# First MLP product of a two-layer backbone: sums moved from GpSimd to VectorE, operand 2 split earlier, context's products put together

## The chip, the core and the metric

The kernel runs on one core of a Trainium2 chip. The metric is the device time of one execution in microseconds; three runs gave 2661.84 to 2663.42, median 2663.18. The core's engines work side by side, each through its own queue in order: TensorE (PE; its weight loads are listed as PEld) multiplies matrices and writes to PSUM, VectorE (DVE) and ScalarE (ACT) do elementwise work, GpSimd (POOL) does elementwise work on SBUF only, and SyncE (SP) issues DMAs. Semaphores order the engines among each other.

## The reference, cut to what matters

Two layers, window attention and gated linear attention, each followed by an MLP, on 1024 latent tokens and, in the first layer, 256 context tokens of width 1024. All is fp32.

```python
def channel_mlp(h, w_in, w_out):
    return jnp.square(jax.nn.relu(h @ w_in)) @ w_out

for i in range(DEPTH):                       # DEPTH = 2
    need_ctx = i < DEPTH - 1
    m_lat = jnp.split((c_lat @ w_mod[i] + b_mod[i])[:, None, :], N_MOD, axis=-1)
    m_ctx = jnp.split(c_con @ w_mod[i] + b_mod[i], N_MOD, axis=-1)
    ...
    x_lat = x_lat + m_lat[2] * rms_norm(y_lat, g_post_mix[i])
    f_lat = channel_mlp(modulate(x_lat, g_pre_mlp[i], m_lat[3], m_lat[4]), w_mlp_in[i], w_mlp_out[i])
    x_lat = x_lat + m_lat[5] * rms_norm(f_lat, g_post_mlp[i])
    if need_ctx:                             # the same for x_ctx
        ...
```

`w_mlp_in[i]` is 1024 x 4096; the product `h @ w_in` is the first MLP product. `modulate` is a norm, a factor and a shift per column.

## The kernel before, in words

**Operands.** An fp32 operand is used in two parts: `split` writes a rounded high part (ScalarE, L213, a cast) and the rest as a low part (VectorE, L214, a subtraction), and `mm3` adds three matmuls, high by high, low by high and high by low (L233 to L235).

**First MLP product** (`mlp_hidden`). The latent tokens are two halves of four tiles of 128, the inner dimension has two halves, and the hidden columns come in 16 blocks `m` of two times 128. Each block is a two-by-two product done with seven products instead of eight. Product `j` (1 to 7) multiplies operand `j` of the activations (`x.ops[j]`, rows `o1` to `o7` of the trace, split once by `MlpIn.apart`) with operand `j` of the weights (rows `wi`, split for each block). Some operands are sums: `sums(m, j)` makes four sums of weight quarters for each block (128x512, L891), on GpSimd; `MlpIn.take` makes those of the activations tile by tile (L131, L132), and `last_sums` turns two operands into sums in place once products 1 and 2 no longer need them (L228 through the helper `sums`: one half on VectorE, the other on GpSimd). A product fills or adds to a PSUM bank (`pa`, `pb`, `pc`). ScalarE copies a bank (L932), VectorE adds another to the copy (L936, an eviction sum), ScalarE applies relu and square (L937, L894).

In layer 0 the context's 256 tokens go through plain products in addition: `x0` for the first 128 columns of a block, `x1` for the second (rows `px`).

**PSUM.** `ps1` has four buffers of one bank; `ps2` has two of two banks, which `y`, `pb`, `px` and, once `tight` is set, the transposes `xt` take in turns. `modulated` transposes a tile on TensorE and evicts the eight 128x128 pieces in turns on ScalarE (L449) and VectorE (L451).

**The entry.** Before the MLP, `mixing` runs over the token tiles: output product `y`, post norm and residual (L462, L463), norm (L429), transposition and modulation (L449, L451), sums (L131, L132). The last tiles of it overlap the first products of the MLP: products 1 and 2 of the first blocks (two blocks in layer 0, three in layer 1) need operands of the first half of the tokens only, product 6 needs the last tile.

**Modulation.** `mod_sums` multiplies `w_mod` by the two conditioning vectors on VectorE: for each 128 rows a tile `wm` of 512 KB is loaded, and each of one or two streams adds to an accumulator `ma` (L313, L315). In layer 0's first MLP product its 56 units are called at even distances.

**What sets the order.** `Timeline` holds a plan: each step is put at a planned time (`tl.at`), a product counting 2.56, and the program is emitted in the order of these times. A scheduler then sets each engine's final order from the emitted one. On the chip each engine takes its queue in that order.

## Time and profile before

| | |
|---|---|
| median of three runs | 2663.18 us |
| the profiled execution | 2665.38 us |
| its span, first to last instruction | 2663.7 us |
| mean granted TensorE clock | 0.988 |
| TensorE busy | 2565.3 us (96%) |
| VectorE busy | 1706.7 us (64%) |
| ScalarE busy | 1258.7 us (47%) |
| GpSimd busy | 638.5 us (24%) |

Layer 0's first MLP product begins at 640.8 us of the span, layer 1's at 2014.4. In a timeline a row gives the start, the duration, the engine, the line, the operation, the tiles written and read, the shape and a count; in brackets stands the idle time of the engine before it and what ended it. Neighbouring instructions overlap by some hundredths of a microsecond, so that the distance of two starts is a little less than a duration. A matmul's row lasts longer than the distance to the next, since they are pipelined. The granted clock is a share of the full rate: 1.00 is the level of 2.4 GHz, 0.50 that of 1.2 GHz.

### The profile page before, as it was taken

The page shows a single profiled execution, that of the slowest core. Times are in us where ns is not written, and L with a number is a line of the kernel's source. Part 1 is how long each engine was busy: PE and PEld are TensorE (multiplying, and loading weights), DVE is VectorE, ACT ScalarE, POOL GpSimd, SP SyncE. Part 2 cuts the span into 40 slices and gives each one's busy share as a digit, 9 for nine tenths or more (in the row PEclk, how much of TensorE's full clock was granted, in tenths as well). Part 3 has the DMA queues.
Part 4 walks back from the last instruction along what each step waited for, and adds up shares of the span by engine and source line. Part 5 has one row for each costly group of instructions (what it writes and reads, how often), then busy time and mean ns, then how long its engine had stood idle before and what let it go on. Part 6 is the DMA issues. An engine that isn't in the chain of part 4 may idle for free. (4 is left out here: it accounts for less than half of the span.)

```text
span 2663.7 us, 36464 instructions
## 1 busy us (share of the span) xinstructions
PE 2565.3 (96%) x13523; PEld 2125.0 (80%) x13523; DVE 1706.7 (64%) x2531; ACT 1258.7 (47%) x2364; POOL 638.5 (24%) x868
## 2 busy tenths in 40 slices
PE   7998999999999999999998999999997999999998
PEld 5777888887788888788776888888786888878787
DVE  4798766657867554866758634736647454478786
ACT  3325777744544444543325544433435454545333
POOL 0355655423223221000001112312414232300002
PEclk9999999999999999999998999999998999999999
DMA  9221000222555654646345322002221434376464
GB/s 305 89 70 40 4 2 25 72 87 74 151 181 172 186 181 147 232 157 226 115 150 197 109 51 91 25 24 95 88 94 42 127 108 114 119 244 212 168 213 166
DMA packets 223523, 329.76 MB, mean 124 GB/s; under 512 B 23897, under 2 KB 122481, under 8 KB 223345
## 3 DMA queue, kind: packets, MB, share of 16 engines
q1 hardware_dynamic: 220752, 318.00, 37.2%
q0 software_dynamic: 2592, 9.44, 0.9%
q8 instruction: 106, 1.74, 0.3%
q14 instruction: 73, 0.59, 0.1%
HBM read 267.60 MB, written 59.77 MB: 123 GB/s over the span
## 5 line engine op out<-in xcount | busy, mean ns | idle before, releaser
L234 PE MATMUL p<-ol,oh 128*128 128x512 f32 x896 | 350.9, 392 | 1.7 <-DVE ol L214 1.7
L235 PE MATMUL p<-oh,ol 128*128 128x512 f32 x896 | 347.1, 391 | 0.0
L233 PE MATMUL p<-oh 128*128 128x512 f32 x896 | 333.0, 394 | 6.7 <-DVE acc L1123 3.7
L246 POOL TENSOR_SCALAR rs<-ss 128x1 f32<-128x1 f32 (+1 forms) x78 | 25.8, 331 | 981.5 <-ACT later L240 796.9
L233 PEld LDWEIGHTS p<-oh 128*128 128x128 f32 x896 | 170.0, 190 | 44.4 <-ACT oh L213 4.7
L234 PEld LDWEIGHTS p<-ol,oh 128*128 128x128 f32 x896 | 169.6, 189 | 38.8 <-DVE ol L214 2.9
L235 PEld LDWEIGHTS p<-oh,ol 128*128 128x128 f32 x896 | 169.3, 189 | 35.5 <-issue 0.2
L315 DVE SCALAR_TENSOR_TENSOR ma<-wm,cT,ma 128x1024 f32<-128x1024 f32 x112 | 162.8, 1486 | 45.1 <-DMA wm<-in_w_mod 44.9
L214 DVE TENSOR_TENSOR ol<-wh,oh 128x1024 fp32r<-128x1024 f32 x128 | 153.7, 1216 | 54.5 <-ACT oh L213 51.3
L214 DVE TENSOR_TENSOR wi<-wi,wi 128x512 fp32r<-128x512 f32 x176 | 154.7, 910 | 49.5 <-ACT wi L213 47.5
L213 ACT CAST oh<-wh 128x1024 fp32r<-128x1024 f32 x128 | 132.4, 1052 | 107.8 <-PE p L235 45.5
L213 ACT CAST oh<-k 128x1024 fp32r<-128x1024 f32 x96 | 98.5, 1053 | 152.4 <-PE p L235 65.3
L932 ACT COPY s<-pa 128x512 f32<-128x512 f32 x96 | 56.1, 586 | 199.4 <-PE pa L235 199.4
L936 DVE TENSOR_TENSOR s<-pc,s 128x512 f32<-128x512 f32 x64 | 43.9, 686 | 162.5 <-ACT s L932 145.5
L710 DVE CUSTOM_DVE_ANT_0 pr<-sc,mask,nsink 128x640 f32<-128x640 f32 (+2 forms) x144 | 108.5, 775 | 42.7 <-PE sc L699 40.9
L214 DVE TENSOR_TENSOR ol<-k,oh 128x1024 fp32r<-128x1024 f32 x96 | 115.4, 1219 | 26.4 <-ACT oh L213 16.4
L715 ACT ACTIVATE pr<-pr,nm 128x640 f32<-128x640 f32 (+2 forms) x160 | 118.6, 742 | 28.1 <-DVE nm L710 25.0
L727 POOL TENSOR_SCALAR pr<-pr,den 128x640 f32<-128x640 f32 (+2 forms) x160 | 118.1, 752 | 36.4 <-PE pt L743 16.8
L235 PE MATMUL y<-woh,ol 128*128 128x512 f32 x288 | 112.5, 391 | 2.8 <-DVE ol L214 2.8
L213 ACT CAST wi<-wi 128x512 fp32r<-128x512 f32 x176 | 102.5, 614 | 26.4 <-DMA hd<-h 7.9
L233 PE MATMUL y<-woh,oh 128*128 128x512 f32 x288 | 114.0, 396 | 0.0
L234 PE MATMUL y<-wol,oh 128*128 128x512 f32 x288 | 112.3, 390 | 0.0
(374 smaller groups left out, 6974.4 us busy)
## 6 DMA issues: line engine op xcount, KB each, us to landing
wm<-in_w_mod SPq DMA_DIRECT2D x96, 512.0 KB, 4.4
wh<-hd SPq DMA_DIRECT2D x160, 256.0 KB, 3.5
wh<-in_w_mlp_out SPq DMA_DIRECT2D x160, 256.0 KB, 4.1
wi<-in_w_mlp_in SPq DMA_DIRECT2D x64, 512.0 KB, 5.6
hd<-h SPq DMA_DIRECT2D x64, 512.0 KB, 3.3
k<-hd SPq DMA_DIRECT2D x64, 256.0 KB, 5.3
k<-in_w_mlp_out SPq DMA_DIRECT2D x64, 256.0 KB, 5.4
x<-in_x SPq DMA_DIRECT2D x16, 512.0 KB, 3.6
```

What stands on the lines that cost most here:

```text
L213: self.nc.scalar.copy(hi, src)
L214: self.nc.vector.tensor_tensor(lo, src, hi.bitcast(F32), op=ALU.subtract)
L233: mm(out, a[0], b[0], start=start, stop=False, skip_group_check=onto)
L234: mm(out, a[0], b[1], start=False, stop=False, skip_group_check=onto)
L235: mm(out, a[1], b[0], start=False, stop=stop, skip_group_check=onto)
L246: nc.gpsimd.tensor_scalar(r, ss, inv_n, EPS, ALU.mult, ALU.add)
L315: nc.vector.scalar_tensor_tensor(acc[s], raw, c, acc[s], ALU.mult, ALU.add)
L710: nc.vector.tensor_tensor_reduce(out=like(pr), in0=like(ps[e][:, off:768]), in1=mask, scale=1.0, scalar=self.nsink[:, c0 + e : c0 + e + 1] ...
L715: nc.scalar.activation(pr, pr, AF.Exp, bias=nm[:, e : e + 1], scale=-1.0, accum_out=sums[:, e : e + 1])
L727: nc.gpsimd.tensor_scalar(probs[e], probs[e], den[:, e : e + 1], 0.0, ALU.mult, ALU.add)
L932: nc.scalar.copy(s["s", j], s["pa"])
L936: nc.vector.tensor_tensor(t, s[bank], t, op=ALU.add)
```

## The change

Six edits. (1) The four weight sums of a block move from GpSimd to VectorE. (2) So do the halves of `last_sums` that ran on GpSimd; the helper `sums` goes. (3) The split of activation operand 2 is planned at `t0 - 7`, ahead of the last tile's tail, where it stood at `at[0, 2] - 6`, which was -0.88 in layer 0 and 1.68 in layer 1. (4) In layer 0, for the first two blocks, `x1` follows `x0` directly and so stands ahead of product 6; for the others it follows product 3 as before. (5) With it the weight operand 3 of these blocks is split in time for `x1`, and sum 4 keeps its place. (6) `mod_sums` gives back control after each stream instead of each unit, so 80 calls replace 56, planned from 36 instead of 30 on.

```diff
@@ MlpIn.last_sums
             if j == 1:
-                kb.sums(c, raw[0, 0][c], m, raw[0, 0][c], ALU.add)
+                kb.nc.vector.tensor_tensor(raw[0, 0][c], m, raw[0, 0][c], op=ALU.add)
             else:
-                kb.sums(c, raw[0, 1][c], raw[0, 1][c], m, ALU.subtract)
+                kb.nc.vector.tensor_tensor(raw[0, 1][c], raw[0, 1][c], m, op=ALU.subtract)
@@ Backbone
-    def sums(self, c, out, a, b, op):
-
-        (self.nc.gpsimd if c else self.nc.vector).tensor_tensor(out, a, b, op=op)
@@ mod_sums
-    def mod_sums(self, vectors):
+    def mod_sums(self, vectors, apart=False):
...
                     nc.vector.scalar_tensor_tensor(acc[s], raw, c, acc[s], ALU.mult, ALU.add)
+                if apart and s + 1 < len(streams):
+                    yield
@@ mlp_hidden
                 full.append((m, j))
-                if full[-1] == (m, j) and j in (1, 2) and (m, 3 - j) in full:
+                if j in (1, 2) and (m, 3 - j) in full:
                     full.append((m, "x0"))
-                if j == 3:
+                    if m < g:
+                        full.append((m, "x1"))
+                if j == 3 and m >= g:
                     full.append((m, "x1"))
...
-            nc.gpsimd.tensor_tensor(out, p, q, op=op)
+            nc.vector.tensor_tensor(out, p, q, op=op)
...
             when = {j: at[m, j] - lead for j in range(1, 8)}
+            if x.ctx:
+                when[3] = min(when[3], at[m, "x1"] - lead)
...
-            tl.at(min(when[4], when[3]) - 2, lambda m=m: sums(m, 4))
+            tl.at(min(when[4], at[m, 3] - lead) - 2, lambda m=m: sums(m, 4))
...
-            tl.at(at[0, 2] - 6, lambda c=c: x.apart(2, c))
+            tl.at(t0 - 7, lambda c=c: x.apart(2, c))
@@ run
-        more = self.mod_sums([(0, 5)] + [(1, j) for j in range(6)])
+        more = self.mod_sums([(0, 5)] + [(1, j) for j in range(6)], True)
...
-        for n in range(56):
-            tl.at(30 + n * (t1 - 60) / 56, lambda: next(more))
+        for n in range(80):
+            tl.at(36 + n * (t1 - 60) / 80, lambda: next(more))
```

Two engines show what this does to the order. In the changed file the lines above the middle are numbered up to four lower, so L449 there is L451 of before, L427 is L429, L311 is L315, and L229 to L231 are L233 to L235. (A name's last number tells buffers apart.)

VectorE in layer 1's entry, before: from the normalisation of the last tile (`xn`) to the fourth VectorE eviction of the transpose buffer `xt_18153` (`q_3247`), whose release product 2 waits for.

```order
L429 TENSOR_SCALAR xn_18174<-xo_18127,rs_18177 128x1024
L214 TENSOR_TENSOR o2l_18182<-q_3182_17564,o2h_18181 128x1024
L214 TENSOR_TENSOR o2l_18186<-q_3183_17565,o2h_18185 128x1024
L214 TENSOR_TENSOR wi_3283_18189<-wi_18023,wi_3283_18189 128x512
L214 TENSOR_TENSOR wi_3286_18207<-wi_18114,wi_3286_18207 128x512
L214 TENSOR_TENSOR wi_3291_18249<-wi_18118,wi_3291_18249 128x512
L214 TENSOR_TENSOR wi_3295_18270<-M_18247,wi_3295_18270 128x512
L451 TENSOR_SCALAR q_3246_17980<-xt_18153,G_10146,S_9703 128x128
L451 TENSOR_SCALAR q_3243_17969<-xt_18225,G_10146,S_9703 128x128
L132 TENSOR_TENSOR qM_17986<-q_3246_17980,q_3243_17969 128x2x128
L131 TENSOR_TENSOR q_3243_17969<-q_3179_17553,q_3243_17969 128x2x128
L451 TENSOR_SCALAR q_3247_17981<-xt_18153,G_10146,S_9703 128x128
```

The same place after the change, up to the same eviction (of `xt_18161`); ahead of the first row stand the normalisation, the splits `wi_3286` and `wi_3291` and one sum (`M_18247`).

```order
L891 TENSOR_TENSOR wi_18023<-wi_18024,M_18247 128x512
L891 TENSOR_TENSOR M_18268<-wi_18115,wi_18114 128x512
L891 TENSOR_TENSOR M_18292<-wi_18119,wi_18118 128x512
L214 TENSOR_TENSOR wi_3295_18270<-M_18247,wi_3295_18270 128x512
L891 TENSOR_TENSOR wi_18114<-wi_18115,M_18268 128x512
L449 TENSOR_SCALAR q_3246_17980<-xt_18161,G_10314,S_10015 128x128
L449 TENSOR_SCALAR q_3243_17969<-xt_18225,G_10314,S_10015 128x128
L891 TENSOR_TENSOR wi_18118<-wi_18119,M_18292 128x512
L891 TENSOR_TENSOR M_18247<-wi_18023,M_18247 128x512
L132 TENSOR_TENSOR qM_17986<-q_3246_17980,q_3243_17969 128x2x128
L131 TENSOR_TENSOR q_3243_17969<-q_3179_17553,q_3243_17969 128x2x128
L449 TENSOR_SCALAR q_3247_17981<-xt_18161,G_10314,S_10015 128x128
```

The two splits of operand 2 have left this stretch, for a place ahead of the evictions of the tile before; the split `wi_3283` stands ahead of the normalisation; seven sums have come in.

TensorE in layer 0's entry, before, at the last tile's transposes (`xt`), which follow product 2 (`pb`) and `x0` (`px`) of the first block:

```order
L235 MATMUL px_7272<-ah_6403,wi_1517_7181 128x256
L441 MATMUL xt_7300<-ident,xn_7222 128x128 x4
L441 MATMUL xt_7309<-ident,xn_7222 128x128 x4
L233 MATMUL pb_7329<-o2h_7173,wi_1527_7244 128x512
L234 MATMUL pb_7329<-o2l_7174,wi_1527_7244 128x512
L235 MATMUL pb_7329<-o2h_7173,wi_1527_7244 128x512
```

And after the change:

```order
L231 MATMUL px_7272<-ah_6403,wi_1517_7181 128x256
L439 MATMUL xt_7297<-ident,xn_7222 128x128 x4
L439 MATMUL xt_7306<-ident,xn_7222 128x128 x4
L229 MATMUL px_7322<-ah_6402,wi_1518_7184 128x256
L230 MATMUL px_7322<-al_6404,wi_1518_7184 128x256
L231 MATMUL px_7322<-ah_6402,wi_1518_7184 128x256
```

Here 24 matmuls of the first block's `x1` have moved in ahead of the second block's product 2; the second block's `x1` follows its `x0`, and product 6 comes after them.

VectorE in layer 0's steady part, before, at a place where four modulation steps stand together ahead of an eviction sum (L936):

```order
L339 TENSOR_TENSOR S_8423<-S_8423,bcol 128x8
L315 SCALAR_TENSOR_TENSOR ma_8450<-wm_8496,cT,ma_8450 128x1024
L315 SCALAR_TENSOR_TENSOR ma_8451<-wm_8496,cT,ma_8451 128x1024
L315 SCALAR_TENSOR_TENSOR ma_8450<-wm_8540,cT,ma_8450 128x1024
L315 SCALAR_TENSOR_TENSOR ma_8451<-wm_8540,cT,ma_8451 128x1024
L936 TENSOR_TENSOR s_1713_8542<-pc_8508,s_1713_8542 128x512
```

And a piece of the same stage after it:

```order
L891 TENSOR_TENSOR wi_7703<-wi_7704,M_7891 128x512
L311 SCALAR_TENSOR_TENSOR ma_7620<-wm_7844,cT,ma_7620 128x1024
L311 SCALAR_TENSOR_TENSOR ma_7621<-wm_7844,cT,ma_7621 128x1024
L936 TENSOR_TENSOR s_1611_7790<-pc_7792,s_1611_7790 128x512
L311 SCALAR_TENSOR_TENSOR ma_7620<-wm_7913,cT,ma_7620 128x1024
L311 SCALAR_TENSOR_TENSOR ma_7621<-wm_7913,cT,ma_7621 128x1024
L936 TENSOR_TENSOR s_1628_7923<-pb_7830,s_1628_7923 128x512
```

In the whole stage the modulation steps now stand alone or in pairs, and the sums stand between them. Outside the two stages the queues are as before, but for some twenty rows at the end of layer 0's second MLP product, where TensorE's last pairs of transposes, and the splits and evictions around them, stand a few rows later or earlier.

## Rows read from the trace of the kernel before

**Rows 1.** The page, busy time by engine: us, share of the span, instructions.

```profile
PE 2565.3 (96%) x13523; PEld 2125.0 (80%) x13523; DVE 1706.7 (64%) x2531; ACT 1258.7 (47%) x2364; POOL 638.5 (24%) x868
```

**Rows 2.** The table by stretches (us from the span's start): length, then busy time and count of PE, PEld, DVE, ACT and POOL, the granted clock, the DMA engines' share and GB/s. Layer 0's entry and steady part, layer 1's entry and steady part, the end of layer 0's second MLP product.

```profile
640.00:702.00 62.00, 54.44 (x265) 44.26 (x266) 55.22 (x63) 38.64 (x68) 25.46 (x18) 0.97 0.27 79
702.00:1040.00 338.00, 332.76 (x1776) 284.39 (x1775) 209.32 (x241) 155.77 (x297) 81.98 (x51) 0.99 0.57 176
2014.00:2060.00 46.00, 32.23 (x125) 25.10 (x126) 38.84 (x44) 26.17 (x45) 22.02 (x15) 0.85 0.03 12
2060.00:2340.00 280.00, 278.82 (x1226) 229.48 (x1225) 127.39 (x152) 144.92 (x262) 79.27 (x52) 1.00 0.40 122
1424.00:1466.00 42.00, 31.19 (x129) 23.74 (x128) 34.41 (x52) 26.53 (x50) 9.12 (x14) 0.84 0.62 214
```

**Rows 3.** The timeline of TensorE in layer 1's entry: the end of product 1, the transposes, and the start of product 2.

```profile
2022.62 0.40 PE L235 MATMUL pa<-o1h,wi 128*128 128x512 f32 x1
2022.85 1.03 PE L441 MATMUL xt<-ident,xn 128*128 128x128 f32 x8
2034.11 0.79 PE L233 MATMUL pb<-o2h,wi 128*128 128x512 f32 x1 [10.22 <-DVE q L451]
```

**Rows 4.** The timeline of VectorE at the same place.

```profile
2019.96 1.78 DVE L429 TENSOR_SCALAR xn<-xo,rs 128x1024 f32<-128x1024 f32 x1 [0.77 <-ACT o2h L213]
2021.66 4.51 DVE L214 TENSOR_TENSOR o2l<-q,o2h 128x1024 fp32r<-128x1024 f32 x2
2026.10 4.01 DVE L214 TENSOR_TENSOR wi<-wi,wi 128x512 fp32r<-128x512 f32 x3
2030.04 0.68 DVE L214 TENSOR_TENSOR wi<-M,wi 128x512 fp32r<-128x512 f32 x1
2030.64 0.72 DVE L451 TENSOR_SCALAR q<-xt,G,S 128x128 f32<-128x128 f32 x2
...
2033.66 0.72 DVE L451 TENSOR_SCALAR q<-xt,G,S 128x128 f32<-128x128 f32 x2
```

**Rows 5.** The timeline of GpSimd at the same place.

```profile
2022.85 4.45 POOL L891 TENSOR_TENSOR M<-wi,wi 128x512 f32<-128x512 f32 x2
2027.26 1.71 POOL L891 TENSOR_TENSOR wi<-wi,M 128x512 f32<-128x512 f32 x1
2030.79 1.27 POOL L891 TENSOR_TENSOR M<-wi,M 128x512 f32<-128x512 f32 x1 [1.83 <-DVE wi L214]
```

**Rows 6.** The table by stretches (columns as in rows 2) at three places where the granted clock falls.

```profile
656.00:660.80 4.80, 4.72 (x15) 3.75 (x16) 3.74 (x7) 4.16 (x10) 3.19 (x3) 0.64 0.09 27
2034.10:2039.20 5.10, 5.09 (x12) 4.02 (x13) 0.94 (x3) 0.00 (x0) 0.00 (x0) 0.50 0.01 3
779.60:783.00 3.40, 3.37 (x8) 2.69 (x9) 1.29 (x2) 2.98 (x6) 0.58 (x1) 0.51 0.00 1
```

**Rows 7.** The timeline of VectorE in layer 0's entry: instructions one after the other.

```profile
633.24 0.75 DVE L429 TENSOR_SCALAR xn<-xo,rs 128x1024 f32<-128x1024 f32 x1 [2.14 <-POOL rs L247]
633.91 0.72 DVE L451 TENSOR_SCALAR q<-xt,G,S 128x128 f32<-128x128 f32 x2
634.55 0.41 DVE L131 TENSOR_TENSOR q<-q,q 128x256 f32<-128x256 f32 x1
634.88 0.41 DVE L451 TENSOR_SCALAR q<-xt,G,S 128x128 f32<-128x128 f32 x1
...
662.75 1.21 DVE L228 TENSOR_TENSOR q<-qM,q 128x1024 f32<-128x1024 f32 x1
663.88 1.21 DVE L228 TENSOR_TENSOR q<-q,qM 128x1024 f32<-128x1024 f32 x1
```

**Rows 8.** The timeline of TensorE in layer 0's entry: the rows with idle time before them, and two neighbouring rows of the context's product.

```profile
656.08 0.50 PE L233 MATMUL pb<-o2h,wi 128*128 128x512 f32 x1 [2.12 <-DVE s L936]
...
661.01 0.28 PE L234 MATMUL px<-al,wi 128*128 128x256 f32 x1
661.13 0.28 PE L235 MATMUL px<-ah,wi 128*128 128x256 f32 x1
...
666.61 0.50 PE L234 MATMUL pa<-o6l,wi 128*128 128x512 f32 x1 [1.14 <-DVE o6l L214]
...
670.52 0.50 PE L234 MATMUL pa<-o6l,wi 128*128 128x512 f32 x1 [0.87 <-DVE o6l L214]
...
674.46 0.50 PE L234 MATMUL pa<-o7l,wi 128*128 128x512 f32 x1 [1.15 <-DVE o7l L214]
```

**Rows 9.** The timelines of VectorE and of TensorE in layer 0's steady part, at two eviction sums.

```profile
770.85 2.48 DVE L315 SCALAR_TENSOR_TENSOR ma<-wm,cT,ma 128x1024 f32<-128x1024 f32 x2 [0.63 <-DMA wm<-in_w_mod]
...
774.45 4.53 DVE L315 SCALAR_TENSOR_TENSOR ma<-wm,cT,ma 128x1024 f32<-128x1024 f32 x2
...
779.63 0.80 PE L233 MATMUL pc<-o3h,wi 128*128 128x512 f32 x1 [2.26 <-DVE s L936]
...
804.21 4.86 DVE L315 SCALAR_TENSOR_TENSOR ma<-wm,cT,ma 128x1024 f32<-128x1024 f32 x4
...
809.72 0.50 PE L233 MATMUL pc<-o3h,wi 128*128 128x512 f32 x1 [1.50 <-DVE s L936]
```

**Rows 10.** Groups of VectorE's instructions by line: count, busy us, mean ns of one, idle time before them and what ended it. The first is of 702 to 1040, the second of 2060 to 2340.

```profile
L315 DVE SCALAR_TENSOR_TENSOR ma<-wm,cT,ma 128x1024 f32<-128x1024 f32 x66 | 95.3, 1470 | 37.6 <-DMA wm<-in_w_mod 37.5
...
L214 DVE TENSOR_TENSOR wi<-wi,wi 128x512 fp32r<-128x512 f32 x70 | 74.3, 1104 | 1.4
```

## Prediction

> **What bounds the kernel now.** I read the page's busy times first: TensorE is busy for 2565.3 of the 2663.7 us, so 98 us of idle time, and what the clock takes, are all that an edit off TensorE can win [rows 1]. Then a table by stretches, for where that idle time lies in the two stages that the change touches: 7.6 us in the entry of layer 0's first MLP product (640 to 702), 5.2 in its steady part, 13.8 in the entry of layer 1's (2014 to 2060), 1.2 in its steady part [rows 2]. That is 27.8 us, the ceiling but for the clock. Then the timelines of TensorE and VectorE at those places. The reader is to see that each long wait there ends with a VectorE instruction, and that VectorE is late because its queue is in order and its instructions are stretched.
>
> In layer 1 TensorE stops at 2023.88, after the second half of a transpose, until 2034.11 [rows 3]. Product 2 takes the PSUM buffer of that transpose, so it waits for the last of the buffer's evictions (L451). Those stand in VectorE's queue behind the split of operand 2 and four weight splits, which take 4.51 and 4.01 us and 0.68 [rows 4], while GpSimd runs sums on the same tiles [rows 5]. When TensorE resumes, the granted clock is 0.50, the 1.2 GHz level, and the 5.1 us of matmuls up to 2039.2 cost half of that, 2.5 us [rows 6].
>
> **The shared port.** A 128x512 split takes 0.68 us alone and two splits of 128x1024 took 4.51 beside GpSimd's sums, against 1.21 for one 128x1024 instruction in layer 0 [rows 4, 7]; GpSimd's two sums took 4.45 meanwhile [rows 5]. The Trainium skill, "SBUF — State Buffer", section "Who interferes with whom", says that a VectorE instruction with two SBUF inputs and a GpSimd instruction that reads SBUF exclude each other for the whole instruction, and that the loser stops. By it the stretched rows fall back to their lone durations once GpSimd is idle, as I assume below; if the stretch came from something else, the two splits would keep 4.5 us. The trace agrees as far as these rows go: the stretched splits lie beside GpSimd's sums, and the one that stands in a pause of them took 0.68 [rows 4, 5].
>
> **The change part by part.**
>
> *a, layer 0's entry.* The losses are four waits, 2.12, 1.14, 0.87 and 1.15 us [rows 8], and 3.4 us at 1.2 GHz around 657 [rows 6], half of it lost: 5.3 + 1.7 = 7.0. The change puts context's second product of the first two blocks, 48 matmuls of 0.12 us (5.8 us) [rows 8], ahead of product 6, and splits operand 2 while VectorE is idle. Walk it. TensorE has 48 matmuls at 0.23 [rows 3], 96 at 0.12 and 16 transposes (two times 1.03) before product 6: 24.6 us from 640.8, so it arrives at 665.4. VectorE's queue from 640.3 to operand 6's first low part holds, by its order: 19 instructions of 128x512 (splits, moved sums, two eviction sums), whose starts lie 0.60 apart, 16 small ones at 0.32 to 0.34, six of 128x1024 at 1.13 and a normalisation at 0.75 [rows 4, 7]. That is 11.4 + 5.3 + 6.8 + 0.75 = 24.2 us, and 1.21 for the low part itself: it is there at 665.7. Nearly even. I leave 1.0 us for two restarts and for VectorE waiting on ScalarE between evictions: a = -6.0. If VectorE loses 2 us to such waits and the clock dips again, -3; at best -7.
>
> *b, layer 0's steady part.* Two waits of 2.26 and 1.50 us, each for an eviction sum (L936) behind modulation steps: two that took 4.53 us, four that took 4.86 [rows 9]. A lone pair takes 2.48, so the first of them lost 4.53 - 2.48 = 2.05 to the stretch [rows 9]. After the change no more than two stand together in the whole stage, by the order, so both waits should nearly go, with the 1.7 us of the clock dip at 779.6 [rows 6]: 2.05 of the one, the 1.50 of the other and 1.7 = 5.2. What is added: four sums in each of 14 blocks, 56 of 0.60, 34 us, minus the stretch of 66 steps (1470 ns against the 1240 of one in the lone pair, 15 us) [rows 9, 10], on an engine that was busy for 209 of 338 us [rows 2]. Busy time fits; order is the question, since an eviction sum may now stand behind a sum and a pair that waits for its weights. The moved step gives its load less time: a load starts after the second stream's step, and by the plan in the code the next step comes 308/80 = 3.85 us later instead of 308/56 = 5.5; the loads make VectorE wait already. I charge 2.2 us for new waits: b = -3.0. Bounds -6.9 (all idle time and the dip) and +4 from here; the larger case is a rival.
>
> *c, layer 1's entry.* VectorE now runs, from the normalisation (L429) to the last eviction that frees the buffer: 0.75, two splits, four sums, a split, a sum, two evictions, two sums, two small ones and the eviction, that is ten at 0.60, two at 0.32, two at 0.34 and 0.41, together 8.5 us, where before it took 14.1 (2019.96 to 2034.07) [rows 4, 7]. One split more and one sum more now stand before the normalisation, 1.2 us, of which the 0.77 us of idle time there takes the larger part [rows 4]. So TensorE resumes between 2028.5 and 2029.6 instead of at 2034.1: 5.0 us. The split of operand 2 saves 4.4, the lone durations and the split that stands earlier save 5.4, and the seven sums in this queue give 4.2 back. The low clock after the wait I leave as it is, since TensorE still stands for about 5 us. Behind it, VectorE's work between the first eviction sum and operand 6's first low part gains two sums of 1.13 (those that GpSimd did, L228) and one of 0.60, and loses the stretch of the splits; I count no change. c = -5.0; bounds -1 (the sums also delay product 1's low parts) and -14 (all idle time of the entry).
>
> *d, layer 1's steady part.* 1.2 us is all there is. 70 splits shrink from 1104 to 680 ns, 30 us, and 56 sums add 34 [rows 4, 10]; VectorE stays near 130 of 280 us [rows 2]. 0, bounds -1 and +2.
>
> *e, the end of layer 0's second product.* The order moves one pair of transposes there by some eight matmuls, in a stretch with 10.8 us of idle time [rows 2]. +1, bounds -1 and +2.
>
> The moved loads are the same in number; GpSimd keeps only the small sums of the norms, and nothing waits for it any more but those.
>
> Sum: -6.0 - 3.0 - 5.0 + 0 + 1.0 = -13.0. The profiled execution took 2665.38 us (its span is 2663.7), 2.2 over the median of the runs, 2663.18. So 2652.4 there, and 2650 as a median.
>
> **Rivals.**
> 1. *Layer 1's wait goes altogether.* For it: the wait is the largest single one, and the split that headed its queue is gone. Against it: seven sums stand where the split stood. It would win the other 5.2 us, the 2.5 us of the slow matmuls and some of the 3.6 us that the entry has beside it (13.8 less 10.2) [rows 2, 3, 6]: 2650 - 11 = 2639.
> 2. *Layer 1 gains nothing* (that part doesn't do what it says). For it: the sums' 4.2 us eat the 4.4 of the split, and the rest goes if the lone durations are not reached. Against it: GpSimd is empty. c = 0 and e at its bound: 2656.
> 3. *VectorE's queue stalls layer 0's steady part; slower.* Mechanism: a modulation step waits for its load at the head of the queue, with sums and an eviction sum behind it. For it: VectorE waits 37.5 us for these loads already [rows 10], and at 779.63 TensorE had no slack left: VectorE's 2.05 us of stretch became 2.26 of wait [rows 9]. Against it: those 37.5 us lie in a part where TensorE stands for 5.2 in all [rows 2]. At 1.5 us in each of 14 blocks it is 21 us, with b's gain gone: 2653 + 21 = 2674. It decides from 0.7 us a block, where 14 blocks eat the 10 us that a, c and e leave.
> 4. *What is won in the entries is given back where other engines limit* (ScalarE's chain, the loads): 2663, within 0.2%.
>
> **How the numbers follow.** Forecast 0.50 (2645 to 2656), rival 1 0.14, rival 2 0.12, rival 4 0.11, rival 3 0.13. The range of 8 in 10 reaches from rival 1 to just over rival 2 and part of rival 4: 2639 to 2661. 0.2% (5.3 us) is about what a measurement of this kernel can tell from no change. Faster than 2657.9: 0.50 + 0.14 + 0.11 of rival 2 = 0.75; slower than 2668.5: 0.12; the rest 0.13.
>
> **What would show it.** In the new profile, between the transposes after product 1 and product 2 in layer 1, a wait of about 5 us that still ends with an eviction; the two splits of operand 2 at 1.2 us each, ahead of the last tile's tail; no split of 128x512 above 0.7 us in either stage; in layer 0 no wait over 1.5 us up to product 7, and waits for eviction sums in the steady part of 2 us in all. A wait of 10 us, or splits that stay at 1.1 us, would make c wrong; waits of more than 1 us in most blocks would make b and the sign wrong.

## The result and the profile after

The changed kernel takes 2642.99 us (median of four runs, 2641.92 to 2645.66), against 2663.30 for the kernel before in the same measurement. The ratio is 0.9919, with a 95% interval of 0.9907 to 0.9932: 20.3 us faster. The prediction was 2650 with a range of 2639 to 2661; the time lies in the range, and the gain is one and a half times the 13 us that were forecast. The profiled execution took 2643.85 us, with a span of 2642.1.

The line numbers of the changed kernel are up to four lower than before behind the removed helper: L235 is now L231, L451 is L449, L429 is L427, L315 is L311; the eviction sum stays on L936 and the splits on L213 and L214.

Ahead of everything else the page's busy times, for [rows 1]:

```profile
PE 2561.1 (97%) x13523; PEld 2124.1 (80%) x13523; DVE 1713.7 (65%) x2663; ACT 1258.3 (48%) x2364; POOL 426.3 (16%) x736
```

GpSimd lost 132 instructions and 212 us of busy time; VectorE took over the 132 and is busy for only 7 us more. That alone says that VectorE's instructions became shorter.

Where the time went is best read from the distance between rows of TensorE that mean the same in both kernels. The two fences hold those rows from the timeline of TensorE (start, duration, engine, line, operation, tiles), first of the kernel before: the first row of product 1 in layer 0, the first row of operand 6 in the third block, the first row of the second MLP product, the first row of product 1 in layer 1, and the first row of that layer's second product. The start of product 2 in layer 1 stands in [rows 3].

```profile
640.80 0.50 PE L233 MATMUL pa<-o1h,wi 128*128 128x512 f32 x1 [1.79 <-ACT wi L213]
...
711.41 0.40 PE L233 MATMUL pa<-o6h,wi 128*128 128x512 f32 x1
...
1068.69 0.39 PE L233 MATMUL px<-oh,ch 128*128 128x512 f32 x1
...
2014.40 0.50 PE L233 MATMUL pa<-o1h,wi 128*128 128x512 f32 x1 [1.71 <-ACT wi L213]
...
2342.67 0.39 PE L233 MATMUL p<-oh 128*128 128x512 f32 x1
```

And of the changed kernel, with the start of product 2 in layer 1 (2013.21):

```profile
639.90 0.50 PE L229 MATMUL pa<-o1h,wi 128*128 128x512 f32 x1 [1.79 <-ACT wi L213]
...
701.67 0.39 PE L229 MATMUL pa<-o6h,wi 128*128 128x512 f32 x1
...
1053.91 0.39 PE L229 MATMUL px<-oh,ch 128*128 128x512 f32 x1
...
1998.86 0.50 PE L229 MATMUL pa<-o1h,wi 128*128 128x512 f32 x1 [1.71 <-ACT wi L213]
...
2013.21 0.79 PE L229 MATMUL pb<-o2h,wi 128*128 128x512 f32 x1 [4.45 <-DVE q L449]
...
2321.76 0.39 PE L229 MATMUL p<-oh 128*128 128x512 f32 x1
```

The differences give four lengths, which the rest of this document uses. "Entry 0" runs from product 1 to operand 6 of the third block; up to there each kernel has done the same context products. "Steady 0" runs from there to the second product, "entry 1" from product 1 to product 2 in layer 1, and "rest 1" from there to layer 1's second product.

| | entry 0 | steady 0 | entry 1 | rest 1 |
|---|---|---|---|---|
| before | 70.6 | 357.3 | 19.7 | 308.6 |
| after | 61.8 | 352.2 | 14.4 | 308.6 |
| difference | -8.8 | -5.0 | -5.4 | 0.0 |

That is 19.2 of the 21.5 us between the two profiled executions (2665.38 and 2643.85). The rest is 0.9 ahead of the first stage and differences of both signs behind it, of up to 2 us, in stages whose work did not change.

How far such a length can be trusted is shown by the kernels below that share a stage's code. Entry 0 is 61.77 to 61.85 us in five of them, entry 1 is 14.35 to 14.42 in four, steady 0 is 350.6 to 352.2 in three, rest 1 is 308.6 to 309.4 in four, and the context rows (`px`) of layer 0's second product span 408.8 to 412.5 over all fourteen. A difference of half a microsecond in the entries is real, and one of a microsecond in steady 0 or rest 1 is not.

**Layer 1's entry.** VectorE's timeline there, for [rows 4]:

```profile
2004.64 0.75 DVE L427 TENSOR_SCALAR xn<-xo,rs 128x1024 f32<-128x1024 f32 x1
2005.30 1.29 DVE L214 TENSOR_TENSOR wi<-wi,wi 128x512 fp32r<-128x512 f32 x2
2006.51 0.69 DVE L891 TENSOR_TENSOR M<-wi,wi 128x512 f32<-128x512 f32 x1
...
2010.24 0.72 DVE L449 TENSOR_SCALAR q<-xt,G,S 128x128 f32<-128x128 f32 x2
...
2012.76 0.72 DVE L449 TENSOR_SCALAR q<-xt,G,S 128x128 f32<-128x128 f32 x2
```

From the normalisation (2004.64) to the row of TensorE that the eviction lets go (2013.21) it now takes 8.6 us; in [rows 3, 4] it took 14.2 (2019.96 to 2034.11). No instruction between them is stretched: the two splits of 128x512 at 2005.30 take 1.29 together, where three took 4.01. The wait of TensorE is still there, is 4.45 us long, and still ends with L449.

**Layer 0.** The rows of TensorE with idle time before them, for [rows 8] and [rows 9]:

```profile
661.94 0.38 PE L229 MATMUL px<-ah,wi 128*128 128x256 f32 x1 [0.47 <-ACT hx L924]
...
666.30 0.50 PE L230 MATMUL pa<-o6l,wi 128*128 128x512 f32 x1 [0.53 <-DVE o6l L214]
...
880.81 0.50 PE L229 MATMUL pc<-o5h,wi 128*128 128x512 f32 x1 [0.89 <-ACT wi L213]
...
937.05 0.50 PE L231 MATMUL pc<-o5h,wi 128*128 128x512 f32 x1 [0.48 <-DVE wi L214]
...
949.59 0.50 PE L229 MATMUL pc<-o3h,wi 128*128 128x512 f32 x1 [1.67 <-DVE s L936]
```

The wait of 2.12 at product 2 is gone with its fall of the clock, and of the three waits for low parts one of 0.53 is left. In the steady part the waits at 779.63 and 809.72 are gone, with the fall of the clock at the first; three others have come, 3.0 us together, later and elsewhere. VectorE's groups (count, busy, mean ns, idle time before), for [rows 10]: the steps in the stretch from 692.6 to 1025, and the weight splits in that from 2044 to 2320:

```profile
L311 DVE SCALAR_TENSOR_TENSOR ma<-wm,cT,ma 128x1024 f32<-128x1024 f32 x69 | 86.8, 1280 | 45.9 <-DMA wm<-in_w_mod 45.9
```

```profile
L214 DVE TENSOR_TENSOR wi<-wi,wi 128x512 fp32r<-128x512 f32 x69 | 44.1, 682 | 1.7 <-ACT wi L213 1.7
```

A modulation step takes 1280 ns where it took 1470, and a weight split 682 where it took 1104. VectorE waits for modulation weights longer than before (45.9 us), and TensorE hardly notices.

### The profile page after: what moved, and what is told of

Its sections match the earlier page's. It is cut to its first block, busy times and chain, and to the rows that moved or that the text cites. A ratio compares the mean times of both kernels' runs of the same rounds, so it can differ in the third digit from the quotient of the medians.

```text
span 2642.1 us, 36265 instructions
## 1 busy us (share of the span) xinstructions
PE 2561.1 (97%) x13523; PEld 2124.1 (80%) x13523; DVE 1713.7 (65%) x2663; ACT 1258.3 (48%) x2364; POOL 426.3 (16%) x736
## 4 chain that ended last, share of the span: by engine, by line
PE 85%; DVE 6%; DMA 4%; ACT 2%; issue 1%; POOL 1%; SPq 1%; DVEq 0%; POOLq 0%; ACTq 0%
PE p L229 7%; PE p L230 7%; PE p L231 7%; PE pa L230 4%; PE pa L231 4%; PE pa L229 4%; PE o L760 3%; PE pt L741 3%; PE y L231 3%; PE y L230 2%; PE y L229 2%; PE rp L229 2%; PE rp L230 2%; PE rp L231 2%; PE pc L229 2%; PE pc L231 2%
## 5 line engine op out<-in xcount | busy, mean ns | idle before, releaser
L230 PE MATMUL p<-ol,oh 128*128 128x512 f32 x896 | 351.0, 392 | 1.5 <-DVE ol L214 1.5
L231 PE MATMUL p<-oh,ol 128*128 128x512 f32 x896 | 346.9, 391 | 0.0
L229 PE MATMUL p<-oh 128*128 128x512 f32 x896 | 332.5, 394 | 6.0 <-DVE acc L1125 4.4
L229 PEld LDWEIGHTS p<-oh 128*128 128x128 f32 x896 | 169.5, 189 | 43.4 <-issue 4.1
L231 PEld LDWEIGHTS p<-oh,ol 128*128 128x128 f32 x896 | 169.3, 189 | 35.6 <-issue 0.2
L214 DVE TENSOR_TENSOR ol<-wh,oh 128x1024 fp32r<-128x1024 f32 x128 | 153.7, 1216 | 53.8 <-ACT oh L213 50.8
L311 DVE SCALAR_TENSOR_TENSOR ma<-wm,cT,ma 128x1024 f32<-128x1024 f32 x112 | 148.9, 1361 | 55.1 <-DMA wm<-in_w_mod 55.1
L213 ACT CAST oh<-wh 128x1024 fp32r<-128x1024 f32 x128 | 132.4, 1053 | 107.9 <-PE p L231 46.4
L213 ACT CAST oh<-k 128x1024 fp32r<-128x1024 f32 x96 | 98.5, 1054 | 150.8 <-DMA k<-in_w_mlp_out 56.1
L214 DVE TENSOR_TENSOR wi<-wi,wi 128x512 fp32r<-128x512 f32 x176 | 115.4, 685 | 48.1 <-ACT wi L213 46.4
L936 DVE TENSOR_TENSOR s<-pc,s 128x512 f32<-128x512 f32 x64 | 43.9, 687 | 145.7 <-ACT s L932 135.9
L214 DVE TENSOR_TENSOR ol<-k,oh 128x1024 fp32r<-128x1024 f32 x96 | 115.5, 1218 | 25.6 <-ACT oh L213 16.9
L213 ACT CAST wi<-wi 128x512 fp32r<-128x512 f32 x176 | 102.3, 614 | 39.4 <-DMA hd<-h 25.1
L231 PE MATMUL y<-woh,ol 128*128 128x512 f32 x288 | 113.1, 393 | 2.8 <-DVE ol L214 2.8
L229 PE MATMUL y<-woh,oh 128*128 128x512 f32 x288 | 114.5, 398 | 0.0
```

The source lines that it names most:

```text
L213: self.nc.scalar.copy(hi, src)
L214: self.nc.vector.tensor_tensor(lo, src, hi.bitcast(F32), op=ALU.subtract)
L229: mm(out, a[0], b[0], start=start, stop=False, skip_group_check=onto)
L230: mm(out, a[0], b[1], start=False, stop=False, skip_group_check=onto)
L231: mm(out, a[1], b[0], start=False, stop=stop, skip_group_check=onto)
L311: nc.vector.scalar_tensor_tensor(acc[s], raw, c, acc[s], ALU.mult, ALU.add)
```

## The experiments

The change has four parts, called here the sums (from GpSimd to VectorE), the early split (of operand 2), the context part (context's second product ahead of product 6 for the first two blocks, with the dates of its weight splits) and the steps (one modulation stream at a time). Four kernels add one part to the kernel before, four take one part out of the changed kernel, and four more ask what the first eight leave open. In the text, differences between kernels are of medians or of stage lengths; the kernel before was timed with each group again (2663.3 to 2665.1), so the ratios compare best. Line numbers differ by some lines between these kernels: an eviction of a transpose is L449 to L453, an eviction sum L934 to L940, a weight sum L889 to L895. All results:

| kernel | median us | ratio to before, 95% interval | entry 0 | steady 0 | entry 1 | rest 1 |
|---|---|---|---|---|---|---|
| after | 2642.99 | 0.9919 (0.9907 to 0.9932) | 61.8 | 352.2 | 14.4 | 308.6 |
| sums alone | 2654.07 | 0.9962 (0.9950 to 0.9974) | 67.8 | 353.4 | 16.7 | 309.1 |
| early split alone | 2659.78 | 0.9980 (0.9971 to 0.9988) | 67.7 | 359.6 | 17.4 | 309.3 |
| context alone | 2661.28 | 0.9987 (0.9978 to 0.9996) | 71.2 | 356.5 | 19.7 | 308.8 |
| steps alone | 2655.81 | 0.9970 (0.9959 to 0.9980) | 68.1 | 350.8 | 19.7 | 308.6 |
| without the sums | 2651.33 | 0.9953 (0.9938 to 0.9967) | 67.2 | 350.7 | 17.4 | 308.2 |
| without the early split | 2648.21 | 0.9937 (0.9924 to 0.9949) | 62.2 | 352.0 | 17.1 | 310.1 |
| without context | 2648.11 | 0.9935 (0.9923 to 0.9948) | 64.0 | 351.6 | 14.4 | 308.6 |
| without the steps | 2643.78 | 0.9921 (0.9909 to 0.9934) | 62.9 | 352.5 | 14.4 | 309.4 |
| unused work on GpSimd | 2650.01 | 0.9943 (0.9930 to 0.9957) | 61.8 | 351.2 | 17.5 | 310.5 |
| later sums in layer 1 | 2642.26 | 0.9913 (0.9900 to 0.9927) | 61.8 | 350.6 | 12.7 | 307.8 |
| GpSimd's sums in steady 0 | 2644.64 | 0.9926 (0.9914 to 0.9938) | 61.9 | 351.3 | 14.4 | 309.4 |
| the last two together | 2642.51 | 0.9916 (0.9903 to 0.9930) | 61.8 | 351.0 | 12.7 | 309.0 |

### The sums alone

```diff
-            nc.gpsimd.tensor_tensor(out, p, q, op=op)
+            nc.vector.tensor_tensor(out, p, q, op=op)
```

(and the same for the half of the last tile's operand sums that GpSimd had).

> The kernel before with only the sums of the first MLP product moved from GpSimd to VectorE; operand 2, context's second product and the modulation steps stay as before. Theory A (the four parts win at separate places, the port and the queue both count): in layer 1 the queue up to the last eviction has two splits at 1.2 and no stretched weight splits, but two sums more, so the wait of 10.2 us falls to 6 to 7.5; layer 0's steady part loses the wait of 2.26 us at 779 and keeps the one of 1.50; layer 0's entry keeps its waits for low parts. Some 8 us in all: 2655. Rival B (all of the gain is the port, and the rest of the change follows from it): nearly the whole 20 us, 2645. Rival C (without the early split the sums eat what the port gives): the wait stays above 9 us, 2661.

2654.07 us: theory A, in the time and in the wait of layer 1, which is 6.76 us:

```profile
2020.64 0.80 PE L229 MATMUL pb<-o2h,wi 128*128 128x512 f32 x1 [6.76 <-DVE q L449]
```

Entry 1 is 3.0 us shorter. In layer 0 it went otherwise than A had it, which let the wait at 779 go and the one at 809 stay: both shrank, to 1.65 and 0.93 us. Ahead of the first the pair of steps now takes its lone 2.48, but two of the moved sums stand in the same queue:

```profile
770.92 0.69 DVE L889 TENSOR_TENSOR wi<-wi 128x512 f32<-128x512 f32 x1
771.52 2.48 DVE L311 SCALAR_TENSOR_TENSOR ma<-wm,cT,ma 128x1024 f32<-128x1024 f32 x2
773.91 0.69 DVE L889 TENSOR_TENSOR M<-wi,wi 128x512 f32<-128x512 f32 x1
774.52 0.69 DVE L934 TENSOR_TENSOR s<-pc,s 128x512 f32<-128x512 f32 x1
```

The fall of the clock did go. Entry 0 is 2.8 us shorter, which A did not expect.

### The early split alone

```diff
-            tl.at(at[0, 2] - 6, lambda c=c: x.apart(2, c))
+            tl.at(t0 - 7, lambda c=c: x.apart(2, c))
```

> The kernel before with only operand 2's split put ahead of the last tile's tail; GpSimd keeps its sums. Theory A: layer 1's wait falls by the 4.5 us that the two splits took, to 5.5 to 6; layer 0's wait of 2.12 us at product 2 goes; together 6.5: 2657. Rival B (the port is all): the splits that remain are stretched as before and fill the place, the wait stays above 8 us, 2661. Rival C (the split is what the queue lacked): the wait falls as in the changed kernel to 4.5 or below, 2656.

2659.78 us, between A and B. These are the waits of layer 1:

```profile
2013.20 0.50 PE L235 MATMUL pa<-o1h,wi 128*128 128x512 f32 x1 [0.92 <-DVE wi L214]
...
2027.90 0.80 PE L233 MATMUL pb<-o2h,wi 128*128 128x512 f32 x1 [6.72 <-DVE q L453]
```

The wait for the buffer fell by 3.5 us to 6.72, and 0.92 of that came back one product earlier: the two long splits now stand ahead of the last tile's tail, and product 1's weight splits come later. Entry 1 gained 2.3. In entry 0 the wait of 2.12 at product 2 went, one of 1.41 for an eviction sum came behind it in the context's product, and 2.9 us were gained in all. In steady 0 2.3 us were lost, mostly by waits of 2.77 and 2.74 us at the two eviction sums. Why those grew isn't shown; the early split has no instruction there, but it moves when TensorE arrives relative to VectorE's queue.

### The context part alone

```diff
                     full.append((m, "x0"))
+                    if m < g:
+                        full.append((m, "x1"))
-                if j == 3:
+                if j == 3 and m >= g:
                     full.append((m, "x1"))
```

(and the dates of product 3's weight splits and of sum 4, as in the change).

> The kernel before with only context's second product of the first two blocks put ahead of product 6. Theory A: the 48 matmuls (5.8 us) cover the three waits for low parts of operands 6 and 7 (1.14, 0.87 and 1.15 us) but not the 2.12 at product 2 with its dip of the clock, nor the steady part: 3 us, 2660. Rival D (context's product is what wins layer 0, since the matmuls fill whatever VectorE is late with): entry down by 6 us or more, 2656. Rival E (the two splits that this needs earlier come ahead of others on VectorE, and the waits only move): no change, 2663.

By the lengths of the profile rival E: entry 0 is 0.6 us longer, steady 0 0.8 shorter. A wait of 2.25 us stands where there was 2.12, and one of 3.02, with the clock at 0.50 behind it, for the three waits for low parts of 1.14, 0.87 and 1.15:

```profile
664.72 0.38 PE L233 MATMUL px<-ah,wi 128*128 128x256 f32 x1 [2.25 <-DVE s L940]
...
671.39 0.79 PE L234 MATMUL pa<-o6l,wi 128*128 128x512 f32 x1 [3.02 <-DVE o6l L214]
```

The reason is on VectorE. The two splits that make operand 6's low parts lie beside GpSimd's sums and take 5.60 us:

```profile
667.96 5.60 DVE L214 TENSOR_TENSOR o6l<-qM,o6h 128x1024 fp32r<-128x1024 f32 x2
```

The 5.8 us of context matmuls are eaten by splits of 2.8 each. The median is 3.0 us lower, with an interval that nearly reaches no change; no stage of the profile shows where that would be, and the profiled execution was the slowest of the eleven (2665.18).

### The steps alone

```diff
-        more = self.mod_sums([(0, 5)] + [(1, j) for j in range(6)])
+        more = self.mod_sums([(0, 5)] + [(1, j) for j in range(6)], True)
-        for n in range(56):
-            tl.at(30 + n * (t1 - 60) / 56, lambda: next(more))
+        for n in range(80):
+            tl.at(36 + n * (t1 - 60) / 80, lambda: next(more))
```

> The kernel before with only the modulation steps taken one stream at a time (80 steps in place of 56). Theory A: two of the three pairs no longer stand together, so the wait of 1.50 us at 809 goes, while the lone pair beside GpSimd still stretches and 1 us or more of the wait at 779 stays with its dip: 1.5 to 2 us, 2661. Rival F (the steps are what the eviction sums waited for, port or not): both waits and the dip go, 5 us, 2658. Rival G (the loads get less time, and steps that wait for them stand ahead of eviction sums): slower, 2668 or more, with waits of over 1 us spread over the blocks.

2655.81 us, 8.5 below before: rival F, and more than it asked for. Both waits and the fall of the clock are gone; the idle time of TensorE in steady 0 is two waits,

```profile
885.90 0.50 PE L233 MATMUL pc<-o5h,wi 128*128 128x512 f32 x1 [0.35 <-ACT wi L213]
...
953.99 0.50 PE L233 MATMUL pc<-o3h,wi 128*128 128x512 f32 x1 [0.57 <-DVE s L938]
```

and entry 0 gained 2.5 us, mostly from waits of 0.26 and 1.22, the second for a weight split that stood behind three steps. GpSimd still runs the sums here, and a step still takes 1442 ns. At the wait of 779 one pair of steps is still ahead of the eviction sum, and still stretched; the pair in front of it is gone:

```profile
773.42 3.51 DVE L315 SCALAR_TENSOR_TENSOR ma<-wm,cT,ma 128x1024 f32<-128x1024 f32 x2
```

So in the steady part spreading the steps is enough by itself, with GpSimd still working beside VectorE.

### Without the steps

The following four edits are against the changed kernel.

```diff
-        more = self.mod_sums([(0, 5)] + [(1, j) for j in range(6)], True)
+        more = self.mod_sums([(0, 5)] + [(1, j) for j in range(6)])
-        for n in range(80):
-            tl.at(36 + n * (t1 - 60) / 80, lambda: next(more))
+        for n in range(56):
+            tl.at(30 + n * (t1 - 60) / 56, lambda: next(more))
```

> The changed kernel with the modulation steps as before (56, both streams of a pair together). From the profiles of the four parts alone: layer 0's first product up to the third block won 8.8 us in the changed kernel, of which the steps alone won 2.5; from there to its end the change won 5.0, the sums alone 3.9 and the steps alone 6.5. Theory H (the parts overlap: the sums and the steps both take away the same waits for eviction sums): only some 2.5 in the entry and 1.2 behind it are lost, 2647. Rival I (the parts add, each has waits of its own): the steps' 9 us are lost, 2652. Rival J (with the sums on VectorE, four steps in a row are a longer obstacle than before): waits for eviction sums of over 2 us in several places, above 2655.

2643.78 us: theory H, and with still less lost than it said (0.8 us in the median, 1.1 in entry 0, 0.2 in steady 0). The steps alone are worth 8.5 us and in company hardly one. The waits at the two eviction sums come back at 1.65 and 0.89 us, without a fall of the clock, and those at 880 to 950 are gone in exchange.

### Without the sums

```diff
-            nc.vector.tensor_tensor(out, p, q, op=op)
+            nc.gpsimd.tensor_tensor(out, p, q, op=op)
```

(and the second half of the last tile's operand sums).

> The changed kernel with the sums back on GpSimd. Theory H (overlap): layer 0's steady part gains 1.4 us, since the steps alone did better there (6.5) than the change (5.0); the entry loses 2.8, layer 1's wait grows by 3.05, as it did between the kernels with one part each: 2647.5. Rival I (the parts add): 6.7 us in layer 0 and 3 in layer 1 are lost, 2653. Rival K (the port is what the other parts need out of the way): the entry of layer 0 falls back by 6 us or more, 2655 or more.

2651.33 us, 8.3 above the changed kernel: between H and I in the time, and by the shares of neither. Entry 1 loses 3.1, as much as H let the wait grow. The wait itself is 4.12 us, no longer than in the changed kernel, since one of 0.82 and rows at 1.2 GHz in product 1 bring TensorE there later. Entry 0 loses 5.5, near K's 6 and twice H's 2.8. VectorE and TensorE at operand 6:

```profile
667.56 5.61 DVE L214 TENSOR_TENSOR o6l<-qM,o6h 128x1024 fp32r<-128x1024 f32 x2
```

```profile
670.99 0.50 PE L234 MATMUL pa<-o6l,wi 128*128 128x512 f32 x1 [3.07 <-DVE o6l L214]
```

This is the picture of the context part alone: as long as GpSimd works beside the splits, the matmuls put ahead buy nothing. Steady 0 is 1.6 us shorter than in the changed kernel, as H had it; but three kernels with the changed kernel's code there differ by as much.

### Without the early split

```diff
-            tl.at(t0 - 7, lambda c=c: x.apart(2, c))
+            tl.at(at[0, 2] - 6, lambda c=c: x.apart(2, c))
```

> The changed kernel with operand 2's split where it was, ahead of product 2. Theory I (the parts add): layer 1's wait grows from 4.45 us by 2.3 (what the early split won alone), layer 0's entry by 2.9; 2648. Rival L (in layer 0 TensorE has nothing to do until the split is there): the entry falls back by 5 us or more, 2651. Rival M (the sums' queue covers the split): the wait in layer 1 stays below 5.5, 2645.

2648.21 us, as theory I said, but by other shares. Entry 1 loses 2.75 us (I: 2.3; its wait is 5.83, not under the 5.5 of rival M), entry 0 only 0.5 instead of 2.9: without GpSimd's sums VectorE's queue doesn't make product 2 wait, even with the two splits at their old place. (In the kernel before, too, these splits were done ten microseconds ahead of product 2; it waited for an eviction sum behind them.) The other 2 us of the median belong to no stage that this part touches, and I don't explain them.

### Without the context part

```diff
-                    if m < g:
-                        full.append((m, "x1"))
-                if j == 3 and m >= g:
+                if j == 3:
                     full.append((m, "x1"))
```

(and product 3's weight splits at their old date).

> The changed kernel with context's second product where it was, behind product 3. Alone the reordering won nothing in the profile (0.2 us in the whole stage). Theory N (it stays worthless: the waits for low parts that it covers only move): 2643, within 2 us. Rival O (it pays once VectorE's queue is short, since then VectorE is ahead after the 5.8 us that it gives): the waits before operands 6 and 7 come back, some 3 us in the entry, 2646. Rival P (it costs, since its weight splits stand ahead of others): 2641 or less.

2648.11 us: rival O, though the wait comes back before operand 6 alone. It is 1.88 us in place of 0.53, and the clock falls behind it, as the row lengths of 0.63 show:

```profile
661.78 0.55 PE L230 MATMUL pa<-o6l,wi 128*128 128x512 f32 x1 [1.88 <-DVE o6l L214]
662.13 0.63 PE L231 MATMUL pa<-o6h,wi 128*128 128x512 f32 x1
```

Entry 0 loses 2.2 us; the other 3 us of the median lie in no stage that this part touches. The same reordering gained nothing in the profile when it stood alone: it pays only once the splits are short.

### Work on GpSimd that nothing uses

```diff
+            for k in 2 * list(range(4 if j in (2, 6) and not x.ctx else 0)):
+                nc.gpsimd.tensor_tensor(self.idle, op[:, 0, k, :].bitcast(F32), self.ident, op=ALU.mult)
```

> The changed kernel with work added on GpSimd that nothing uses: in layer 1's first product, behind each cast of a block's weights for products 2 and 6, eight products of 128x128 of the cast tile and a constant. VectorE's, ScalarE's and TensorE's order is the same as in the changed kernel, and nothing waits for GpSimd there. Theory Q (the port: VectorE's two-input instructions stop while GpSimd works on SBUF): the 128x512 splits and sums in layer 1's entry go from 0.68 us to 1 or more, the wait of 4.45 us to 6.5 or more, and the time to 2645 to 2650. Rival R (the stretch came from the tiles that both engines shared in the kernel before): rows stay at 0.68 and the wait at 4.45, 2643.

Theory Q. The wait grows from 4.45 to 7.57 us, entry 1 by 3.1, rest 1 by 1.9, and the median is 7.0 above the changed kernel's. First the rows of VectorE, then one of GpSimd, then TensorE's wait:

```profile
2006.58 0.96 DVE L429 TENSOR_SCALAR xn<-xo,rs 128x1024 f32<-128x1024 f32 x1
2007.45 1.82 DVE L214 TENSOR_TENSOR wi<-wi,wi 128x512 fp32r<-128x512 f32 x2
2009.20 0.95 DVE L895 TENSOR_TENSOR M<-wi,wi 128x512 f32<-128x512 f32 x1
...
2014.37 0.72 DVE L451 TENSOR_SCALAR q<-xt,G,S 128x128 f32<-128x128 f32 x2
2015.01 0.83 DVE L895 TENSOR_TENSOR wi<-wi,M 128x512 f32<-128x512 f32 x1
...
2016.63 0.67 DVE L132 TENSOR_TENSOR qM<-q,q 128x256 f32<-128x256 f32 x1
```

```profile
2014.84 0.46 POOL L881 TENSOR_TENSOR idle<-wi,ident 128x128 f32<-128x128 f32 x1
```

```profile
2018.26 0.79 PE L229 MATMUL pb<-o2h,wi 128*128 128x512 f32 x1 [7.57 <-DVE q L451]
```

No other engine waits for these products, and no tile is written by both engines. Yet a 128x512 sum goes from 0.69 to between 0.83 and 0.95 us (theory Q had asked for 1 or more, for longer GpSimd instructions than these), one of 128x256 from 0.41 to 0.67. Two evictions (L451), which read PSUM, take 0.72 as ever, and the GpSimd product beside them takes 0.46. The normalisation and the 128x256 sums touch no tile that these products read. So the stretch comes with GpSimd's work on SBUF, not with shared tiles; rival R falls.

### The sums later in layer 1

```diff
-                tl.at(when[6] - 3, lambda m=m, j=j: sums(m, j))
+                tl.at(when[6] - (3 if x.ctx or m >= g else -2), lambda m=m, j=j: sums(m, j))
```

(with the split and the sum that follow them 2.5 later for the same blocks).

> The changed kernel with the sums of layer 1's first three blocks asked for 5 us later, so that two sums, a split and a small sum that stood ahead of the last freeing eviction on VectorE now stand behind it; the rest is the same. Theory A (the remaining wait of 4.45 us is the length of that queue): it falls by 1.5 to 2 us, to about 2.7, and product 6 does not come later; 2641.5. Rival S (the sums are missed behind it: product 6 waits longer for its operand by as much): 2643. Rival T (a shorter wait also spares a stretch at 1.2 GHz): 2639.5.

The wait fell by 1.65 us, and product 6's own wait is 1.81 us, as it was (1.86); A, and not S. (By the rows one sum, the split and the small sum now stand behind the eviction, not two sums.)

```profile
2006.83 0.50 PE L229 MATMUL pb<-o2h,wi 128*128 128x512 f32 x1 [2.80 <-DVE q L449]
2007.16 0.40 PE L230 MATMUL pb<-o2l,wi 128*128 128x512 f32 x1
```

The rows after it are at 2.4 GHz (0.40), where after the wait of 4.45 they took 0.63. Entry 1 is 1.7 us shorter. Rival T's gain comes only in part, since the clock falls for longer further on: it is 0.50 for 6.0 us from 2019.6, at operand 6, where in the changed kernel it is 0.53 for 5.2 us from 2013.2 and 0.51 for 3.5 us from 2028.3. The median, 2642.26, is 0.7 below the changed kernel's: the two intervals overlap for the most part, so that this version is faster is not shown.

### GpSimd's sums in layer 0's steady part, and both edits

```diff
-            nc.vector.tensor_tensor(out, p, q, op=op)
+            (nc.gpsimd if x.ctx and m >= g else nc.vector).tensor_tensor(out, p, q, op=op)
```

> The changed kernel with the sums of layer 0's steady part (from the third block on) back on GpSimd; layer 0's first two blocks and layer 1 keep them on VectorE. Theory H (the steady part owes its gain to the steps alone, and the sums cost it 1.5 us): from the third block to the end of the product 350.7 us in place of 352.2, as in the run with all sums on GpSimd; 2641.5. Rival I (the sums help in the steady part too): 353 us or more there, 2644 or more.

> Both edits together: the sums of layer 0's steady part on GpSimd, and the sums of layer 1's first three blocks later. They lie in separate stages, so by theories A and H they add: 1.5 + 1.7 below the changed kernel, 2640. Rival: one of the two gains nothing, 2641.5; both give nothing, 2643.

With GpSimd's sums steady 0 is 351.3 us, in the middle of what the changed kernel's own code gives there (350.6 to 352.2); the medians are 2644.64 and 2642.51. Neither the gain of 1.5 us that H promised nor the loss of rival I is shown: where the steps are spread, it makes no difference that this stage can show on which engine its sums run. Entry 1 gains its 1.7 us in the second kernel again. No version clearly beats the changed kernel.

## Why the prediction was right, and where it was too small

**Layer 1's entry (c, -5.0): right, by its own steps.** Walked from the rows' lone durations, VectorE's queue was to take 8.5 us from the normalisation to the freeing eviction; it takes 8.6. TensorE was to resume 14.1 to 15.2 us after the start of product 1, and resumes after 14.4. The measured term is -5.4. That it is made of two halves is shown by the single parts, -3.0 for the sums and -2.3 for the early split, and taking either out loses 3.1 and 2.75. The lone durations, on which the walk rested, were reached: no 128x512 split of either stage takes more than 0.70. The Trainium skill, "SBUF — State Buffer", section "Who interferes with whom", also says that a VectorE instruction with at most one SBUF input stays clear of GpSimd, unless it runs in a mode that uses both ports. The evictions of 0.72 beside the unused products agree; the normalisation, which has one SBUF tensor as input, went from 0.75 to 0.96 there, and whether it runs in such a mode no row shows. Rivals 1 and 2 fall: the wait of 10.2 us became one of 4.45, neither 0 nor 10. By the time alone rival 1 (2639) lies nearer to 2643 than the forecast; it is this row that decides.

**Layer 0's entry (a, -6.0): the mechanism right, the term too small; it measured -8.8.** The walk itself was close: operand 6's low part was to be ready 24.9 us after the start of product 1, and TensorE waits for it until 26.4 (666.30 less 639.90), 0.5 us beyond the 1.0 that I had left for such losses. What I mis-sized is the loss of before. I summed four waits and the clock, 7.0. The idle rows up to the third block fell by 5.8 us, since two waits of 0.26 and 1.22, at 690 and 698, went too; the kernel with the steps alone loses them as well, and my term left the steps out. The clock gave its 1.7, as [rows 6] had it, and the remaining 1.3 are what a wait costs beyond its own row (below). The walk held because it put the lone durations in: with stretched splits, as two experiments show, the context part that I gave the credit to buys nothing. In the changed kernel it is worth 2.2 us, and the sums 5.5.

**Layer 0's steady part (b, -3.0): the two waits and the clock went, as said; it measured -5.0.** The charge of 2.2 us for new waits was fair: 3.0 of them came, in three places. The gain was counted too low, since four further waits (0.23, 0.25, 0.27 and 0.73) and the cost of restarting went as well. One step of the argument was too narrow: I ascribed the wait at 779 to the 2.05 us by which GpSimd stretched the pair. The kernel with the steps alone keeps a stretched pair there (3.51) and loses the wait; the one with the sums alone loses the stretch and keeps a wait of 1.65, behind two of the moved sums. Either part alone wins 3.9 us or more in this stage, so that the steps are worth 8.5 us alone and 0.8 in company. My sum took them as one term and did not see that they overlap.

**Layer 1's steady part (d, 0): right**, 308.6 in both for all that follows product 2's start. **The end of layer 0's second product (e, +1): not shown**; the second product is 2.0 us shorter in the profile, but it varies by 3.7 us among kernels that have the same work there.

**Rival 3, the slower one,** asked for waits of 1.5 us in each block. VectorE does wait longer for the modulation weights (45.9 us), but TensorE's three waits of steady 0 are 3.0 us: its slack in a block is large enough. Rival 4 falls with the sum of the stages. The prediction's signs came as named: operand 2's splits take 1.22 us each (at 1992.04 and 1994.41), no wait of layer 0 between product 1's first row and product 7 is over 0.53, and the one wait for an eviction sum in the steady part is 1.67.

So with the three measured stages the terms a, b and c are -19.2 where they were forecast at -14.0, and no run shows the +1 of e.

## What to carry to other kernels

Before moving work off a busy engine or onto it, read whether its rows are stretched by a neighbour: VectorE took 132 instructions more and the kernel became faster, since a weight split beside GpSimd's sums had taken 1104 ns as a mean in layer 1, and takes 682 without them. Parts of a change that remove the same wait must not be added, and one that hides a late operand was worth nothing here until the operand's own work was short; it takes both kernels, the one with a part alone and the one without it, to see this. When a wait ends with an in-order queue, count that queue's rows from the last common point at their lone durations: that was right to 0.1 us in layer 1's entry, and 1.5 us too short in layer 0's.

## What the runs showed of the hardware

Which VectorE instructions GpSimd slows shows in one kernel: two SBUF inputs (0.69 to 0.95, 0.41 to 0.67) and the 128x1024 normalisation from SBUF (0.75 to 0.96) stretch, evictions from PSUM don't. The loss is mutual: a GpSimd product that takes 0.46 us beside an eviction takes 669 ns as a mean over all 256 of them:

```profile
L881 POOL TENSOR_TENSOR idle<-wi,ident 128x128 f32<-128x128 f32 x256 | 171.2, 669 | 136.4 <-ACT wi L213 117.5
```

A wait of TensorE costs more than its row says. At the wait of 1.22 in the kernel before, the row ahead of it began 1.50 us earlier, where a row of its kind (128x256) is followed after 0.12, and the next one came after another 0.34, where these (128x512) are followed after 0.23: 1.38 and 0.11 lost, 0.27 more than the row says. The other waits of entry 0 between two matmuls at 2.4 GHz show the same, 0.27 to 0.28. Six waits became two; with some restarts whose idle time is too short for a row this makes 1.3 of entry 0's 8.8 us.

```profile
697.00 0.28 PE L234 MATMUL px<-al,wi 128*128 128x256 f32 x1
698.50 0.50 PE L235 MATMUL pa<-o4h,wi 128*128 128x512 f32 x1 [1.22 <-DVE wi L214]
698.83 0.40 PE L233 MATMUL pa<-o4h,wi 128*128 128x512 f32 x1
```

And the length of a wait alone can mislead. In the kernel without the steps, and in the one with GpSimd's sums in steady 0, TensorE waits for product 2 in layer 1 for 3.19 us, not 4.45, with the same instructions on VectorE. Entry 1 is 14.4 us in all three: the clock had fallen earlier, in product 1 (rows of 0.63), TensorE came later, and VectorE set the end.
